# Softmax division on either of two engines, and a new order of work, in a hybrid RWKV / sliding-window attention step

## The chip, the cores and the metric

The kernel runs on one core of a Trainium2 chip. The metric is the time of one launch on the device in microseconds (us), the median of the runs. The engines are called as the profile calls them: PE (TensorE, matrix products; PEld its weight loads), DVE (VectorE), ACT (ScalarE), POOL (GpSimd) and SP (SyncE, which issues the DMAs).

## What is computed

One layer of a decoder, for a prompt of 2048 tokens and for eight single-token samples that share the weights. Cut to what matters:

```
mod = silu(c) @ w_ada + b_ada ; shift, scale, gate = split(mod, 3)
h = rms_norm(x) * (1 + scale) + shift
u = h @ w_in                                  # r, k, v, lora, z, q, k, v, two gates
o_a = rwkv(r, k, v, decay, a)                 # state recurrence in chunks of 64 tokens
logits = q @ k.T / 8 + bias(dist), masked to a window of 128
m = max(max(logits), sink) ; p = exp(logits - m)
probs = p / (sum(p) + exp(sink - m))          # the softmax with a sink
o_b = probs @ v
merged = sigmoid(g_a) * ((o_a * silu(z_a)) @ w_o_a) + sigmoid(g_b) * ((o_b * silu(z_b)) @ w_o_b)
y = x + gate * (merged @ w_out)
```

## The kernel before

The 2048 tokens are worked off in four quarters of 512 (`q` is 0 to 3; here first to fourth quarter). The eight samples ride along in the second. In a quarter, `make_h` norms the input (of the next quarter, ahead of time), `dense` makes each 128 columns of `h @ w_in` (a weight is split into two parts, and three products of 128x128 by 512 stand for one exact product), `rwkv_group` does the recurrence for two groups of heads (`half` 0 and 1: `prep_pair`, `inverses`, then a chain of eight chunk steps), `attention` works four blocks of 128 queries (`attend`), and `merge` and `finish` close the quarter. `STAGES` says in which order a quarter takes its two groups and the attention.

Ahead of it all, `ada` makes `mod` in six groups of 512 columns, four of them before the first quarter (`ADA`). A group takes eight loads of `w_ada` of 256 KB. Where its flag is False, each load is split by a cast (ACT or DVE) and a subtraction (DVE), and PE makes two products of 18x512 in the short form. Where it is True, PE multiplies the whole fp32 load with a 9-column operand, which it does in two records, and neither ACT nor DVE touches the load. Four small transposing products and an addition on DVE finish a group; `make_h` needs the groups 0 and 2 for its first half and 1 and 3 for its second.

The order of work is no loop order. The program records every operation with a key, and `schedule` places them before the build: for each engine, in turn, the ready operation with the smallest key. The key is six times the count of dense steps so far, less a lead from `LEADS` (a row per kind of work, eight numbers for the quarters and halves). Each engine then executes its list strictly in that order, so an operation that waits holds up all behind it. An operation may name two engines (`copy` names ACT and DVE, many products DVE and POOL), and `schedule` then takes the one that it finds free first. On PE, `schedule` prefers among ready products one that uses the array as the last one did, within `NEAR` units of key.

In `attend`, DVE adds the bias and takes the maximum (L1273), ACT takes eight exponentials with their sums (L1285), DVE inverts the sum, and then multiplies the eight 128x256 tiles by it (L1290, `ts`, always DVE). PE transposes the result (L1297), copies follow (L1299), and PE multiplies by the values (L1302).

Of the kernel before, what the change touches and what calls it, by code (L numbers as in the profile page):

```python
# [13 lines left out]
AF = mybir.ActivationFunctionType  # L14
ALU = mybir.AluOpType
# [72 lines left out]
def _constants():  # L88
# [19 lines left out]
CAPS = {"p": 92, "s": 11, "t": 14,  "nl": 1, "d": 3, "g": 5}  # L108
LEADS = {
    "prep": (2813.7, 2813.7, 2813.7, 3436.9, 2813.7, 2813.7, 3438.6, 2813.7),  # L110
    "inv": (2996.9, 2996.1, 5811.5, 5811.5, 3844.5, 4038.1, 3844.5, 3844.5),
    "chain": (1123.8, 1097.6, 888.3, 1123.8, 2826.9, 888.3, 888.3, 1097.6),
    "gn": (2855.6, 3576.9, 3664.2, 4278.9, 4097.0, 4097.0, 3576.9, 4278.9),
    "wd": (2660.8, 2660.8, 451.6, 3265.3, 1897.4, 1897.4, 1897.4, 1897.4),
    "norm": (6898.3, 3392.1, 820.0, 988.1, 462.2, 462.2, 838.5, 462.2),
    "att": (4680.1, 4566.4, 4726.2, 4726.2, 4352.4, 4352.4, 4902.9, 4642.8),
    "sample": (1353.8, 3662.2, 1353.8, 3662.2, 1353.8, 3662.2, 3662.2, 1353.8),
    "bias": (4326.4, 4447.3, 4335.8, 2812.3, 1723.9, 4335.8, 4355.1, 2812.3),
    "h": (3270.3, 3142.9, 3267.4, 3267.4, 3533.2, 3372.5, 3372.5, 3267.4),
    "x": (390.0, 390.0, 427.3, 427.3, 456.5, 456.5, 395.2, 427.3),  # L120
}
WLEAD, ELEAD = 5000.0, 6000.0
HGATE = 4
ADA = ((0, False), (1, True), (2, False), (3, False))
EARLY, PLACE = 1, 3
INORDER = 24
STAGES = ('0A1', '01A', '0A1', '0A1')
# [151 lines left out]
SWITCH = 50  # L279
FULL_ARRAY = (128, 128)  # L280
TURN = (0.09, 0.19)
NEAR = 300
AHEAD = 2
PE_LAT = 0.23

# [1 line left out]
def schedule(prog):  # L287
# [68 lines left out]
    def pick(e):  # L356
        T = free[e]
        best = None
        for x in ready[e]:
# [23 lines left out]
            if t <= T + 1e-9:  # L383
                if e == "pe" and table[1] not in (None, FULL_ARRAY, o.table[0]):
                    for y in ready[e]:
                        if y[0] > x[0] + NEAR:
                            break
# [87 lines left out]
def _free_size(v):  # L475
    n = 1
    for x in v.shape[1:]:
        n *= x
    return n


def _cost(e, op, out, ins, kw):
    n = _free_size(out)
    psum = any(v.buf.kind in ("d", "g") for v in ins)
    ptr = sum(1 for v in ins[1:] if _free_size(v) == 1 and n > 1)
    if e == "dve":
        if op == "tensor_mul" and any(len(v.ap.ap) > 2 and v.ap.ap[-1][0] >= 16 for v in ins):
            return 0.07 + n * 0.00178
        if op == "tensor_tensor_scan":
            return 0.07 + n * 0.00208  # L490
        if op in ("tensor_copy", "memset", "tensor_scalar"):
            return 0.067 + n * (0.00104 if psum else 0.00052) + 0.061 * ptr * (op == "tensor_scalar")
        if op == "tensor_reduce":
            return 0.07 + _free_size(ins[0]) * 0.00104
        if op == "reciprocal":
            return 0.07 + n * 0.0063
        return 0.07 + n * 0.00104 + 0.061 * ptr * (op == "scalar_tensor_tensor")
    if e == "act":
        return (0.052 if psum else 0.094) + n * 0.000833 + 0.093 * (len(ins) - 1 + ("accum_out" in kw))
    if op == "memset":  # L500
        return 0.035 + n * 0.00084
    if op == "tensor_scalar":
        return 0.147 + n * 0.0034
    if op == "tensor_copy":
        return 0.14 + n * 0.0008
    return 0.147 + n * 0.0022
# [3 lines left out]
def hybrid_step_kernel(ctx: ExitStack, tc: tile.TileContext, A, O):  # L510
    nc = tc.nc
# [4 lines left out]
    pr = Program(A["xT"].tensor, caps)  # L516
# [7 lines left out]
    def res(x):  # L524
        return x.real() if isinstance(x, View) else x
# [3 lines left out]
    def do(engs, op, out, /, *a, **k):  # L529

        if isinstance(engs, str):
            engs = {e: op for e in engs.split("/")}
        outs = [out] + ([k["accum_out"]] if "accum_out" in k else [])
        ins = [x for x in (*a, *(v for n_, v in k.items() if n_ != "accum_out")) if isinstance(x, View)]
        table = None
        if op == "activation":
            table = {AF.Ln: 5, AF.Exp: 0, AF.Tanh: 0}.get(a[1])
        o = pr.rec({e: _cost(e, n_, out, ins, k) for e, n_ in engs.items()},
                   lambda e: getattr(ENG[e], engs[e])(res(out), *(res(x) for x in a), **{n_: res(v) for n_, v in k.items()}),  # L539
                   outs, ins, table=table)  # L540
        if op in ("tensor_reduce", "memset", "transpose"):
            o.port = False
# [7 lines left out]
    def add(out, a, b, engs="dve"):  # L550
        do(engs, "tensor_add", out, a, b)
# [4 lines left out]
    def ts(out, in_, s1, s2, op0, op1=None, engs="dve"):  # L556
        k = {} if op1 is None else {"op1": op1}
        do(engs, "tensor_scalar", out, in_, s1, s2, op0=op0, **k)

    def stt(out, a, s, b, op0, op1):  # L560
        do("dve", "scalar_tensor_tensor", out, a, s, b, op0=op0, op1=op1)

    def act(out, in_, f, scale=1.0, bias=0.0, **k):
        do("act", "activation", out, in_, f, bias=bias, scale=scale, **k)
# [52 lines left out]
    def P(shape, dt=F32):  # L617
        return pr.tile("p", shape, dt)

    def Sm(shape):  # L620
        return pr.tile("s" if math.prod(shape[1:]) > 16 else "t", shape)

    def G(shape):
        return pr.tile("g", shape)
# [618 lines left out]
    def attend(q, n, qn, kk, kprev, vt, bt, zb):  # L1243
        k0 = 128 if (q == 0 and n == 0) else 0
        nk = 256 - k0
        lg = [[P([128, 2, 256]) for _ in range(2)] for _ in range(2)]
        mx = Sm([128, 8])
        for p2 in range(2):
            pss = [G([128, 2, 256]) for _ in range(2)]
            calls = []  # L1250
            for p in range(2):
                for g, h in enumerate((lo, hi)):
                    qs = qn[2 * p2 + p][g][:, n * 128:(n + 1) * 128]
                    if n == 0:
                        parts = [(kk, slice(0, 128), slice(128 - k0, 256 - k0))]
                        if q > 0:
                            parts.append((kprev, slice(0, 128), slice(0, 128)))
                    else:
                        parts = [(kk, slice(n * 128 - 128, n * 128 + 128), slice(0, 256))]
                    for t, cols, to in parts:  # L1260
                        calls.append((pss[g][:, p, to], qs, t[g][:, cols], dict(start=True, stop=False)))
                        calls.append((pss[g][:, p, to], qs, t[2 + g][:, cols], dict(start=False, stop=True)))
            mms(calls)
            for p in range(2):
                for g in range(2):
                    h = 4 * g + 2 * p2 + p
                    do("dve", "tensor_tensor_reduce", lg[g][p2][:, p, 0:nk], in0=pss[g][:, p, 0:nk],
                       in1=bt[g][p2][:, p, k0:256], scale=1.0, scalar=-3e38, op0=ALU.add, op1=ALU.max,
                       accum_out=mx[:, h:h + 1])
        do("dve", "tensor_max", mx, mx, vc("sinks", 0, 8))  # L1270
        nmx = Sm([128, 8])
        ts(nmx, mx, -1.0, None, ALU.mult)
        es = Sm([128, 8])  # L1273
        add(es, nmx, vc("sinks", 0, 8))
        act(es, es, AF.Exp)
        den = Sm([128, 8])
        for h in range(8):
            x = lg[h // 4][h % 4 // 2][:, h % 2, 0:nk]
            act(x, x, AF.Exp, bias=nmx[:, h:h + 1], accum_out=den[:, h:h + 1])
        add(den, den, es)  # L1280
        do("dve", "reciprocal", den, den)
        for h in range(8):
            x = lg[h // 4][h % 4 // 2][:, h % 2, 0:nk]
            ts(x, x, den[:, h:h + 1], None, ALU.mult)
        ops = G([128, 4, 128])  # L1285
        for kb in range(k0 // 128, 2):
            ptss = []
            for g in range(2):
                pt = G([128, 4, 128])
                for p in range(4):  # L1290
                    tr(pt[:, p, :], lg[g][p // 2][:, p % 2, kb * 128 - k0:kb * 128 - k0 + 128], ident)
                pts = P([128, 4, 128])
                copy(pts, pt)
                ptss.append(pts)
            v = vprev if n + kb == 0 else vt[:, n + kb - 1]
            mms([(ops[h], v[:, h], ptss[g], dict(start=(kb == k0 // 128), stop=(kb == 1)))
                 for g, h in enumerate((lo, hi))])  # L1297
        for p in range(4):
            y = zb[p][:, n * 128:n * 128 + 128]  # L1299
            mul(y, ops[:, p, :], y)  # L1300
# [236 lines left out]
    early = {}  # L1537
    for g, whole in ADA:
        if g == ADA[PLACE][0]:
            early = {key: weights("w_in", INDEX[key], "dve") for key in ORDER[:EARLY]}  # L1540
# [3 lines left out]
    for q in range(NQ):  # L1544
        sample = q == SQ
# [5 lines left out]
        x = shifted(("wd", 0))  # L1551
# [183 lines left out]
```

## Time and profile before

| | us |
|---|---|
| median of 3 runs | 1837.15 |
| lowest and highest of them | 1836.59, 1839.27 |
| profiled execution, own time | 1840.68 |
| its span | 1838.9 |

| engine | busy us | share |
|---|---|---|
| PE | 1785.1 | 97% |
| DVE | 1293.6 | 70% |
| ACT | 806.7 | 44% |
| POOL | 112.7 | 6% |

A busy PE is read with care: ends of products are modelled, and a product that runs at half clock or waits inside the pipeline counts as busy as well. What a stretch costs is better read from the distance between starts.

### The profile page before, as it was taken

The page shows a single profiled execution, that of the slowest core. Times are in us where ns is not written, and L with a number is a line of the kernel's source. Part 1 is how long each engine was busy: PE and PEld are TensorE (multiplying, and loading weights), DVE is VectorE, ACT ScalarE, POOL GpSimd, SP SyncE. Part 2 cuts the span into 40 slices and gives each one's busy share as a digit, 9 for nine tenths or more (in the row PEclk, how much of TensorE's full clock was granted, in tenths as well). Part 3 has the DMA queues.
Part 4 walks back from the last instruction along what each step waited for, and adds up shares of the span by engine and source line. Part 5 has one row for each costly group of instructions (what it writes and reads, how often), then busy time and mean ns, then how long its engine had stood idle before and what let it go on. Part 6 is the DMA issues. An engine that isn't in the chain of part 4 may idle for free.

```text
span 1838.9 us, 34113 instructions
## 1 busy us (share of the span) xinstructions
PE 1785.1 (97%) x12544; PEld 1436.3 (78%) x12544; DVE 1293.6 (70%) x3160; ACT 806.7 (44%) x1690; POOL 112.7 (6%) x191
## 2 busy tenths in 40 slices
PE   6999999999999998999999999999999999999999
PEld 2777766777898987999997786686888787777787
DVE  8989989587389967957527799673733879873251
ACT  6687645462263756235005765513303567431300
POOL 0100310000011100000000001100000100100000
PEclk9999999999999999999999999999999999999999
DMA  9677575858944534575465543445829263364626
GB/s 333 214 233 254 184 227 188 274 190 292 327 161 124 165 94 123 175 228 177 162 214 177 182 139 104 140 158 180 288 88 310 73 218 91 97 204 150 221 109 201
DMA packets 238933, 343.34 MB, mean 187 GB/s; under 512 B 73981, under 2 KB 77742, under 8 KB 238764
## 3 DMA queue, kind: packets, MB, share of 16 engines
q1 hardware_dynamic: 238764, 341.14, 56.4%
q8 instruction: 99, 1.62, 0.4%
q14 instruction: 70, 0.57, 0.1%
HBM read 263.09 MB, written 77.96 MB: 185 GB/s over the span
## 4 chain that ended last, share of the span: by engine, by line
PE 62%; DVE 13%; ACT 5%; DMA 3%; issue 2%; SPq 0%; DVEq 0%; ACTq 0%
PE d L580 50%; DVE p L539 12%; PE g L598 7%; ACT p L539 3%; PE g L580 3%; PE g L605 2%; ACT L539 2%; DMA p<-lo_w_in 1%; DMA d<-p 0%; DMA p<-in_lora 0%; SPq L614 0%; DMA p<-lo_w_out 0%; DVE s L539 0%; DMA p<-in_w_o 0%; DMA nl<-d 0%
## 5 line engine op out<-in xcount | busy, mean ns | idle before, releaser
L580 PE MATMUL d<-p,p 128*128 128x512 f32 (+2 forms) x7176 | 1475.5, 356 | 17.3 <-ACT p L539 14.9
L580 PEld LDWEIGHTS d<-p,p 128*128 128x128 f32 (+1 forms) x7176 | 1145.1, 188 | 229.5 <-ACT p L539 16.5
L539 DVE TENSOR_TENSOR p<-p,p 128x512 fp32r<-128x512 f32 (+6 forms) x702 | 429.0, 638 | 43.8 <-ACT p L539 35.2
L539 ACT CAST p<-p 128x512 fp32r<-128x512 f32 (+3 forms) x310 | 182.3, 613 | 161.8 <-DVE p L539 85.4
L598 PE MATMUL g<-p,p 128*64 128x64 f32 (+5 forms) x4000 | 230.5, 241 | 8.9 <-DVE p L539 5.0
L598 PEld LDWEIGHTS g<-p,p 128*64 128x64 f32 (+4 forms) x4000 | 175.1, 140 | 74.5 <-issue 20.6
L539 ACT COPY p<-g 64x128 f32<-64x128 f32 (+4 forms) x359 | 130.6, 372 | 150.9 <-PE g L598 78.9
L539 ACT ACTIVATE p<-d,vec 128x511 f32<-128x511 f32 (+1 forms) x65 | 39.2, 603 | 250.9 <-PE d L580 249.4
L539 ACT ACT_TABLE_LOAD x107 | 137.3, 1283 | 19.4 <-PE g L580 16.8
L539 ACT ACTIVATE p<-d 128x512 f32<-128x512 f32 (+1 forms) x120 | 61.4, 512 | 172.3 <-PE d L580 166.5
L539 DVE SCALAR_TENSOR_TENSOR p<-p,d 128x512 f32<-128x512 f32 (+1 forms) x120 | 69.6, 580 | 85.5 <-PE d L580 81.8
L539 DVE TENSOR_TENSOR p<-p,nl 128x2 f32<-128x2 f32 (+30 forms) x248 | 126.4, 510 | 4.4
L539 DVE SCALAR_TENSOR_TENSOR p<-d,modt,p 128x512 f32<-128x512 f32 (+2 forms) x40 | 25.8, 644 | 132.0 <-PE d L580 125.3
L539 DVE TENSOR_TENSOR p<-g,s 64x128 f32<-64x128 f32 (+1 forms) x124 | 40.4, 326 | 97.2 <-PE g L598 93.2
L539 ACT ACTIVATE p<-p 128x512 f32<-128x512 f32 (+2 forms) x161 | 98.1, 631 | 13.9 <-DVE p L539 7.3
L539 DVE TENSOR_TENSOR p<-g,cst 64x256 f32<-64x256 f32 (+1 forms) x192 | 89.5, 506 | 5.2 <-PE g L598 4.2
L539 DVE TENSOR_REDUCE p<-p 128x15 f32<-128x450 f32 (+30 forms) x252 | 88.9, 354 | 4.3
L580 PE MATMUL g<-p,blocks 128*128 128x512 f32 x204 | 80.5, 425 | 9.6 <-DVE p L539 5.8
L605 PE MATMUL g<-cst,p 128*128 128x128 f32 (+1 forms) x457 | 72.7, 282 | 10.2 <-DVE p L539 9.1
L539 POOL TENSOR_TENSOR p<-p,p 64x256 f32<-64x256 f32 (+2 forms) x49 | 56.0, 1154 | 375.8 <-DVE p L539 225.0
L605 PEld LDWEIGHTS g<-cst,p 128*128 128x128 f32 (+1 forms) x457 | 53.6, 143 | 32.6 <-DVE p L539 15.3
L539 ACT ACTIVATE p<-p,t 128x256 f32<-128x256 f32 (+1 forms) x129 | 63.0, 493 | 9.7 <-DVE t L539 9.6
(139 smaller groups left out, 901.2 us busy)
## 6 DMA issues: line engine op xcount, KB each, us to landing
p<-hi_w_in SPq DMA_DIRECT2D x258, 256.0 KB, 5.1
p<-lo_w_in SPq DMA_DIRECT2D x258, 256.0 KB, 5.3
p<-in_w_in SPq DMA_DIRECT2D x86, 256.0 KB, 3.8
hi_w_in<-p SPq DMA_DIRECT2D x86, 256.0 KB, 2.9
lo_w_in<-p SPq DMA_DIRECT2D x86, 256.0 KB, 2.6
p<-in_xT SPq DMA_DIRECT2D x64, 256.0 KB, 5.3
p<-in_w_ada SPq DMA_DIRECT2D x48, 256.0 KB, 5.3
p<-hi_w_o SPq DMA_DIRECT2D x48, 256.0 KB, 5.3
```

Of the source, the lines that this page charges most:

```text
L539: lambda e: getattr(ENG[e], engs[e])(res(out), *(res(x) for x in a), **{n_: res(v) for n_, v in k.items()}),
L580: pr.rec({"pe": mm_cost(out, lhsT, rhs)}, lambda e: nc.tensor.matmul(res(out), res(lhsT), res(rhs), **k), [out], [lhsT, rhs], table=(part( ...
L598: nc.tensor.matmul(res(out), res(lhsT), res(rhs), **k)
L605: pr.rec({"pe": 2 * _free_size(in_) / 2400.0 + 0.003}, lambda e: nc.tensor.transpose(res(out), res(in_), res(idn)), [out], [in_, idn], tab ...
```

## The change

The eight multiplications of `attend` by the inverted sum may now run on ACT as well as on DVE (`scaled`); the flag of two of the four early `ada` groups is True where it was False; `NEAR` is 4000 where it was 300; and 27 of the 88 numbers in `LEADS` are others, of which one row stands here.

```diff
 LEADS = {
...
-    "chain": (1123.8, 1097.6, 888.3, 1123.8, 2826.9, 888.3, 888.3, 1097.6),
+    "chain": (1123.8, 1208.2, 888.3, 1123.8, 609.1, 609.1, 888.3, 1097.6),
...
-ADA = ((0, False), (1, True), (2, False), (3, False))
+ADA = ((0, True), (1, True), (2, False), (3, True))
...
-NEAR = 300
+NEAR = 4000
...
+    def scaled(out, in_, s):
+
+        run_ = {"act": lambda: nc.scalar.activation(res(out), res(in_), AF.Copy, scale=res(s)),
+                "dve": lambda: nc.vector.tensor_scalar(res(out), res(in_), res(s), None, op0=ALU.mult)}
+        pr.rec({"act": _cost("act", "activation", out, [in_, s], {}), "dve": _cost("dve", "tensor_scalar", out, [in_, s], {})},
+               lambda e: run_[e](), [out], [in_, s])
...
         for h in range(8):
             x = lg[h // 4][h % 4 // 2][:, h % 2, 0:nk]
-            ts(x, x, den[:, h:h + 1], None, ALU.mult)
+            scaled(x, x, den[:, h:h + 1])
```

Lines from L560 on are seven higher in the changed kernel (L580 is L587, L598 L605, L605 L612). Of the 128 divisions, 45 come to ACT and 83 stay on DVE; PE goes from one shape of the array to another 539 times where it did 552 times.

The first place is PE's list at the start. `p_13` and `p_12` are the two forms of the conditioning operand (18 and 9 columns), `blocks` is the operand of the norm's sum in `make_h`. Before:

```order
L580 MATMUL d_209<-p_39_326,p_13_260 18x512
L580 MATMUL g_212<-p_41_330,blocks 128x512
L580 MATMUL d_209<-p_45_337,p_13_260 18x512
L580 MATMUL d_209<-p_43_334,p_13_260 18x512
L580 MATMUL g_212<-p_48_342,blocks 128x512
L580 MATMUL d_209<-p_52_352,p_13_260 18x512
```

Now:

```order
L587 MATMUL d_209<-p_15_268,p_12_256 9x512
L587 MATMUL d_209<-p_17_274,p_12_256 9x512
L587 MATMUL g_212<-p_41_329,blocks 128x512
L587 MATMUL g_212<-p_43_334,blocks 128x512
L587 MATMUL d_209<-p_19_279,p_12_256 9x512
L587 MATMUL d_209<-p_21_283,p_12_256 9x512
```

Groups 0, 1 and 3 are now whole products (9x512), and two of them stand ahead of both products of the norm.

The second place is ACT's list in the first quarter, where `inverses` of group 0 ends. The tiles of 32x512 and 32x8x32 are its copies (L1109 and L1115), for which PE waits; the casts of 128x512 split a weight that a DMA has just loaded. Before:

```order
L539 ACTIVATE p_614_2714<-d_210 128x512
L539 COPY p_590_2585<-g_214 128x512
L539 CAST p_623_2785<-p_615_2718 128x512
L539 CAST p_625_2792<-p_618_2727 128x512
L539 COPY p_627_2799<-g_215 32x512 x2
L539 COPY p_585_2558<-g_214 32x8x32
```

Now:

```order
L539 CAST p_580_2628<-p_571_2584 128x512
L539 ACTIVATE p_582_2636<-d_210 128x512
L539 COPY p_587_2678<-g_213 32x512 x2
L539 CAST p_594_2739<-p_585_2673 128x512
L539 COPY p_544_2444<-g_215 32x8x32
```

The two casts of the next weight stood ahead of the copies of 32x512; now the copies stand ahead of both.

The third place is PE's list in the third quarter, in the chain of chunk steps of group 0. Products of 64x64 are the chain, those of 128x512 dense work. Before, the end of a step and the start of the next:

```order
L598 MATMUL g_214<-p_2197_11609,p_2243_11849 64x64
L580 MATMUL d_211<-p_1947_10087,p_2488_13001 128x512
L580 MATMUL d_211<-p_1953_10123,p_2486_12994 128x512
L580 MATMUL d_211<-p_1955_10135,p_2486_12994 128x512
L580 MATMUL d_211<-p_1953_10123,p_2488_13001 128x512
L580 MATMUL d_211<-p_1959_10156,p_2486_12994 128x512
L580 MATMUL d_211<-p_1961_10170,p_2486_12994 128x512
L598 MATMUL g_214<-p_2196_11605,p_2205_11648 64x64
```

Now, the last dense products ahead of the start of a step:

```order
L587 MATMUL d_209<-p_1943_10173,p_2382_12595 128x512
L587 MATMUL d_209<-p_1945_10179,p_2380_12587 128x512
L587 MATMUL d_209<-p_1948_10193,p_2380_12587 128x512
L587 MATMUL d_209<-p_1945_10179,p_2382_12595 128x512
L587 MATMUL d_210<-p_1919_10035,p_2429_12888 128x512
L605 MATMUL g_216<-p_2164_11525,p_2173_11568 64x64
```

Six products of 128x512 stood between the two steps. Now 24 of them stand there (two with `blocks`, the norm's sum) and four transposes; at the ends of the next two steps 11 and 7 of them stand, where 4 stood.

## Rows read from the trace of the kernel before

**Rows 1.** The page: busy time of each engine, share of the span, instructions.

```profile
PE 1785.1 (97%) x12544; PEld 1436.3 (78%) x12544; DVE 1293.6 (70%) x3160; ACT 806.7 (44%) x1690; POOL 112.7 (6%) x191
```

**Rows 2.** Waits of PE, whole span: for whom, us in total, times, longest.

```profile
PE d L580 <- ACT p L539: 14.9, 3, 13.7
PE g L605 <- DVE p L539: 9.1, 10, 3.4
```

**Rows 3.** Chain that ended last: start, us, what; a stretch of dense products.

```profile
1722.02 112.73 PE d L580 x486
```

**Rows 4.** Groups by line and shape, softmax: count, busy us, mean ns, idle before.

```profile
L539 ACT ACTIVATE p<-p,t 128x256 f32<-128x256 f32 x120 | 59.5, 501 | 7.7 <-DVE t L539 7.5
...
L539 DVE TENSOR_SCALAR p<-p,t 128x256 f32<-128x256 f32 x120 | 34.2, 358 | 3.9 <-issue 3.8
```

**Rows 5.** Timeline from 0 to 75 us: start, us, engine, instruction, [idle before].

```profile
5.92 17.34 SPq L614 DMA_DIRECT2D p<-in_w_ada  x24
...
13.65 0.61 PE L580 MATMUL d<-p,p 128*18 128x512 f32 x1 [13.65 <-ACT p L539]
...
17.76 0.15 PEld L580 LDWEIGHTS d<-p,p 128*18 128x18 f32 x1 [0.28 <-DVE p L539]
...
18.19 0.15 PEld L580 LDWEIGHTS d<-p,p 128*18 128x18 f32 x1 [0.28 <-issue]
...
24.93 5.25 SPq L614 DMA_DIRECT2D p<-in_w_ada  x8
...
26.03 0.09 PEld L580 LDWEIGHTS d<-p,p 128*9 128x9 f32 x1 [0.34 <-issue]
26.46 0.09 PEld L580 LDWEIGHTS d<-p,p 128*9 128x9 f32 x1 [0.34 <-DMA p<-in_w_ada]
...
30.95 3.47 PE L580 MATMUL d<-p,p 128*18 128x512 f32 x14
...
44.62 1.05 PE L580 MATMUL g<-cst,p 18*128 18x9 f32 x8 [0.51 <-ACT p L539]
...
46.86 10.93 PE L580 MATMUL d<-p,p 128*128 128x512 f32 x46
```

**Rows 6.** The page, DMA issues: count, KB each, us from issue to landing.

```profile
p<-in_w_ada SPq DMA_DIRECT2D x48, 256.0 KB, 5.3
```

**Rows 7.** Timeline from 236 to 250 us, end of the inverses, first quarter.

```profile
239.75 1.65 PE L580 MATMUL d<-p,p 128*128 128x512 f32 x6
...
241.41 1.32 ACT L539 CAST p<-p 128x512 fp32r<-128x512 f32 x2 [4.56 <-DMA p<-in_w_in]
...
243.39 0.24 PE L598 MATMUL g<-p,p 32*32 32x32 f32 x2 [1.99 <-ACT p L539]
...
245.83 2.93 PE L580 MATMUL d<-p,p 128*128 128x512 f32 x6
```

**Rows 8.** Stretches: from:to, us, busy by engine (instructions), PEclk, DMA share, GB/s.

```profile
248.00:250.00 2.00, 2.00 (x8) 1.60 (x8) 1.97 (x8) 0.35 (x1) 0.00 (x0) 0.50 0.92 298
...
736.40:738.40 2.00, 2.00 (x11) 2.00 (x10) 2.00 (x7) 1.07 (x2) 0.00 (x0) 0.50 0.91 327
```

**Rows 9.** Timeline at 735 us, attention of the second quarter.

```profile
735.32 0.32 DVE L539 TENSOR_SCALAR p<-p,t 128x256 f32<-128x256 f32 x1 [3.79 <-issue]
735.34 0.09 DVE L539 MEMSET nl<- 128x32 f32 x1
...
735.69 1.11 PE L605 MATMUL g<-cst,p 128*128 128x128 f32 x4 [3.40 <-DVE p L539]
```

**Rows 10.** Timeline of PE from 80 to 113 us, first quarter.

```profile
90.94 0.74 PE L580 MATMUL g<-p,blocks 128*128 128x512 f32 x2 [1.53 <-DVE p L539]
```

**Rows 11.** Waits of PE from 1130 to 1180 us, third quarter.

```profile
PE g L598 <- DVE p L539: 3.1, 4, 1.5
PE g L605 <- DVE p L539: 1.0, 1, 1.0
```

**Rows 12.** Stretch in the attention of the third quarter, columns as in Rows 8.

```profile
1080.00:1100.00 20.00, 20.00 (x117) 16.74 (x117) 19.74 (x78) 12.60 (x48) 0.00 (x0) 1.00 0.29 93
```

More of the change, by code (lines that the diff above doesn't have):

```diff
@@ L110 @@
     "prep": (2813.7, 2813.7, 2813.7, 3436.9, 2813.7, 2813.7, 3438.6, 2813.7),
-    "inv": (2996.9, 2996.1, 5811.5, 5811.5, 3844.5, 4038.1, 3844.5, 3844.5),
-    "chain": (1123.8, 1097.6, 888.3, 1123.8, 2826.9, 888.3, 888.3, 1097.6),
-    "gn": (2855.6, 3576.9, 3664.2, 4278.9, 4097.0, 4097.0, 3576.9, 4278.9),
-    "wd": (2660.8, 2660.8, 451.6, 3265.3, 1897.4, 1897.4, 1897.4, 1897.4),
+    "inv": (2996.9, 2996.1, 5293.6, 5811.5, 5293.6, 4038.1, 5293.6, 5293.6),
+    "chain": (1123.8, 1208.2, 888.3, 1123.8, 609.1, 609.1, 888.3, 1097.6),
+    "gn": (3022.4, 3132.6, 3097.4, 3132.6, 3925.1, 3925.1, 3925.1, 3925.1),
+    "wd": (2660.8, 2660.8, 377.1, 377.1, 1897.4, 1897.4, 1897.4, 1897.4),
     "norm": (6898.3, 3392.1, 820.0, 988.1, 462.2, 462.2, 838.5, 462.2),
     "att": (4680.1, 4566.4, 4726.2, 4726.2, 4352.4, 4352.4, 4902.9, 4642.8),
[L117 to L120, printed above, removed]
+    "sample": (1353.8, 2341.0, 1353.8, 3662.2, 1353.8, 3662.2, 3662.2, 1353.8),
+    "bias": (4342.2, 4342.2, 4335.8, 2812.3, 1693.8, 1693.8, 1693.8, 2812.3),
+    "h": (4519.0, 4519.0, 3267.4, 3267.4, 3533.2, 3372.5, 3372.5, 3267.4),
+    "x": (390.0, 390.0, 427.3, 427.3, 462.2, 456.5, 395.2, 462.2),
 }
```

## Prediction

> **What bounds the kernel.** I read the page first: PE is busy 97% of the span, DVE 70%, ACT 44% [rows 1]. So time is won only where PE stands or runs slowly, or where it gets fewer or cheaper products. The waits of PE come next: they are small, 14.9 us for ACT (of which 13.7 is the first product's) and 9.1 us at the transposing products for DVE in ten waits [rows 2]. The chain that ended last then gives the price of dense work: 486 products of 128x512 take 112.73 us, 0.232 each [rows 3]. A stall costs more than its own length: behind the two stalls that I looked at, the stretches show a granted clock of 0.50, the 1.2 GHz level, in place of 1.00, 2.4 GHz [rows 8]. The change is therefore worth what it does to single stalls, and I found these by laying PE's new order beside the timeline of before.
>
> **The divisions.** Of 128, 45 go to ACT. On DVE one takes 0.358 us alone [rows 4] and 0.28 in a run (1.40 for five [rows 9]). ACT's price for a division is in no row; the nearest is its exponential with a sum on the same tile, 0.501 [rows 4], which I take, as the division has the same read and write and no sum. It may lie between 0.28, as fast as DVE, and 0.501. In a block of eight, some three go to ACT (1.5 us) while five stay on DVE (1.4 us), where eight took 2.2: the path from exponentials to transposes is some 0.8 us shorter. In 16 blocks that is 13 us, but PE has dense work to do meanwhile: all its waits for DVE at transposing products are 9.1 us [rows 2], so nearly all of it is hidden and I cost the division itself at 0. Without that cover, if divisions queue behind exponentials, PE waits; that is E below. The terms follow, in order of time.
>
> **T1, the start: +3.4 us (−1 to +6.2).** Two groups become whole products. Split, 14 records take 3.47 us [rows 5], so 16 take 4.0. A whole record starts 0.43 after the one before (26.03 and 26.46 [rows 5]), two make one product of 0.86, eight make 6.9. That is 3 us more for a group, 6 for two; PE's extra is at most 6.2 (with the split at 3.8). What is removed, 16 casts and 16 subtractions, PE did wait for there: 0.28 for DVE at 17.76, with records 0.43 apart, not 0.25 [rows 5]; and the first product waits to 13.65 for a cast, where a whole product needs the load alone. The loads are issued 0.72 apart from 5.92 on (17.34 for 24) and land 5.3 after issue [rows 5, 6]: the first at 12 to 13, the last early one (issue 24.93 + 5.25, landing 5.3 later) at 35.5. So PE, not the loads, paces the new start: from 13.0, 24 whole products at 0.86 (20.6), 16 split records (3.8), two norm sums (0.5), three sets of transposing products at 1.05 (3.2) and some 2 us for early products at half speed make 43.1; the bias and two dense products bring it to 44.3, and the row that the last set transposes comes from a copy now on DVE, at some 45. Then the last set ends at 46.3. Before it ended at 44.62 + 1.05 = 45.67, by when 12 more dense products had been made, 2.8 us. So +0.6 + 2.8 = +3.4. The low end is a start of PE at 12 and no cold products, the high one all of the extra products uncovered.
>
> **T2, shapes of the array: −1.5 (0 to −3.0).** There are 13 fewer switches. No row prices one; they cost from nothing to the slot of a dense product, 0.232 [rows 3]. I take half.
>
> **T3, first quarter, end of the inverses: −4.5 (−5 to 0).** Two casts for which a DMA is late hold ACT idle 4.56 us and end at 242.7; the copies that PE needs stand behind them, so PE waits 1.99 at 243.39 [rows 7] (and some 0.4 beside it). The clock is then 0.50 [rows 8], and six dense products take 2.93 where the same six took 1.65 before the stall [rows 7]; over the 6.6 us to 250 about 2.5 is lost so, if all of it was at half clock. 1.99 + 0.4 + 2.5 is 4.9. The new order has the copies ahead of both casts. What is late next is the weight itself: the dense products behind need those casts. They stand further behind, so I leave 0.4 for that.
>
> **T4, first quarter, 87 to 113 us: −2.0 (−3.4 to 0).** PE waits 1.53 at 90.94 [rows 10] for the squares of the next input's norm. With five smaller waits I count 3.4. The lead of `h` puts 11.1 us of PE work, at the prices of T1 and rows 3, where 7.9 stood between the matching operations; I take 60% of it.
>
> **T5, second quarter's attention: −2.0 (−4.8 to +1).** DVE stands 3.79 us [rows 9]: its list has the memset of `nl` ahead of six divisions (the two labels at 735.32 and 735.34 read as swapped), and that memset waits for the DMAs that write out what `nl` held. PE waits 3.40, and its clock is 0.50 after it [rows 8, 9]: together 4.8, with 1.4 for the 2.8 us at half clock. In the new list the divisions precede the memset, but a subtraction that a norm's product needs stands right behind it, with 0.5 us of PE work in hand. The wait thus mostly moves. I take 40% of the gain; a longer wait at the new place gives the +1.
>
> **T6, third quarter's chain: −3 (−4.7 to 0).** From 1130 to 1180 PE waits 3.1 us in the chain and 1.0 at transposes [rows 11], and a little for ACT. With 24, 11 and 7 products of 0.232 between steps in place of 6 and 4, the waits on the first steps are covered. These products are taken from elsewhere, so I leave a third.
>
> **T7, new waits: +4 (0 to +14).** In the second halves of the third and fourth quarter DVE is full: 19.74 of 20 us [rows 12]. There the PE work between a block's logits and its transposes falls from some 18 to 13 us in the new order, in four blocks. 16.74 of those 20 us are PE's [rows 12], so PE has some slack already; I take 1 us a block.
>
> **The sum:** 3.4 − 1.5 − 4.5 − 2.0 − 2.0 − 3 + 4 = −5.6. The profiled execution's 1840.68 becomes 1835.1; the median of the runs is 3.5 under the profiled one, so I forecast **1831.6**. A measurement of this kernel tells about 0.2%, 3.7 us, from no change.
>
> **The rivals.**
> - **A**, the forecast: −5.6, chance 0.47. T3 speaks for it most: its cause can be read in a row, and the order that makes it is gone.
> - **D**, no new waits: T7 is 0, as DVE is rid of 45 × 0.28 = 13 us; −9.6, 1827.5. If the gains of T5 and T6 also come whole (−2.8, −1.7), 1823. For it speaks the shorter path of a block; against it DVE's 19.74 of 20 [rows 12]. 0.13.
> - **C**, no change that can be told: the start takes all of +6.2, and the memset's wait re-forms whole (T5 is 0): −5.6 + 2.8 + 2.0 = −0.8, 1836.3. This is also the case where the option does little, as 83 of 128 divisions stay and PE never waited for most of them. For it: PE paces the new start. Against it: 16 subtractions less on DVE there. 0.26.
> - **E**, slower: in those four blocks the divisions on ACT stand behind the exponentials and copies in ACT's list (ACT has 12.60 of 20 already [rows 12]), and the cover that fell by 5 us is no longer enough. The price is up to 5 us a block, 20 in all; at 3.5 a block T7 is 14, the sum is −9.6 + 14 = +4.4, 1841.6. It decides from 13.3 us on, 3.3 a block. For it: the cut in cover is in the order. Against it: ACT has 7 of 20 us free there. 0.14.
>
> The Trainium skill (page "ScalarE: Activation LUTs", section "Rules for kernel authors") says that a multiplication belongs on VectorE and not on ScalarE; the tile's rows, 0.501 on ACT for an exponential against 0.358 on DVE [rows 4], agree in direction. By that rule alone, with 45 × 0.14 = 6.4 us all on the path, the forecast would be +0.8, 1838.0; I count it under E, since ACT is the engine with room.
>
> **How the numbers follow.** Faster by over 0.2% holds A and D, 0.60; within it C, 0.26; slower E, 0.14. The range goes from D with its whole gains, 1823, to just short of E, 1841. A's own range, with T5, T6 and T7 off by some 1 each (1.7 together), is 1829.9 to 1833.3.
>
> **What would show it.** T1: eight more pairs of 9x512 in each of two groups, and the last set of transposing products of the start ends near 46.3. T3: no wait near 2 us at the 32x32 products that end the inverses, and a clock of 1.00 behind it. T5: no wait of 3.4 at the transposes of the second quarter, perhaps one at a norm's product instead. T6: less than 2 us of waits for DVE in the third quarter's chain. T7: transposing products (now L612) that wait under 2 us each for DVE or ACT in the third and fourth quarter. The prediction is wrong if the sum of PE's waits does not fall, if a new stall with a clock of 0.50 behind it appears, or if the last early set ends after 50.

## The result, and the profile after

The changed kernel takes 1851.59 us (median of 4 runs, 1849.97 to 1853.26), beside 1838.21 for the kernel before in the same comparison. The ratio on record is 1.0064: 0.64% slower, with an interval of 0.52 to 0.77%; the two medians by themselves lie 13.4 us apart. The forecast was 1831.6, faster, with a range to 1841: wrong in sign and outside its range. The profiled execution takes 1852.02, its span 1850.0, 11.1 us more than before; the profiled execution of the kernel before, at 1840.68, was 2.5 us above the median.

The page, busy time of each engine (before: [rows 1]):

```profile
PE 1792.8 (97%) x12544; PEld 1440.6 (78%) x12544; DVE 1287.0 (70%) x3142; ACT 804.0 (43%) x1689; POOL 103.5 (6%) x178
```

PE is busy for 7.7 us longer, DVE 6.6 us less. ACT is busy no longer although it has 45 divisions more: by the two pages, 18 casts (most of them of the two `ada` groups) and 28 copies fewer run on it. PE's waits sum to 50.4 us where they summed to 47.6; a second profile (`a_again`, below) has 53.1. Shares of busy time tell nothing of the cause here.

To find the place, I laid the traces side by side. Each has 4520 PE records of 128x128 by 512 (dense work, and the norm's sums), and the n-th of one is set against the n-th of the other. Between the rows the order differs, so that only rows at the end of a stage, where both have done the same work, are read. Differences of start to the kernel before in us, with the sum of the prediction's forecasts for its terms up to there (T2 left out) and, in the last column, a second profile of the changed kernel from the experiments:

| at (us, before) | stage that ends | changed | terms | changed, again |
|---|---|---|---|---|
| 78 | start | +2.35 | +3.4 (T1) | +3.28 |
| 221 | first quarter, early | +0.49 | +1.4 (T4) | +1.22 |
| 510 | first quarter | −0.29 | −3.1 (T3) | −0.13 |
| 985 | second quarter | +7.65 | −5.1 (T5) | +5.27 |
| 1071 | third, before its second half | +6.22 | −5.1 | +3.85 |
| 1474 | third quarter | +8.11 | −6.1 (T6, half of T7) | +5.86 |
| 1830 | end | +11.08 | −4.1 (half of T7) | +8.80 |

So the whole loss arises behind the first quarter. The largest step lies at 735 us, at the memset of `nl` that T5 speaks of. The timeline of the changed kernel there (DVE, PE, and SP's loads of `nl`):

```profile
726.30 0.43 DVE L539 CAST p<-p 128x512 fp32r<-128x512 f32 x1 [2.40 <-ACT p L539]
736.62 0.66 DVE L539 TENSOR_TENSOR p<-p,p 128x512 fp32r<-128x512 f32 x1 [9.89 <-issue]
736.64 0.09 DVE L539 MEMSET nl<- 128x32 f32 x1
...
727.02 0.73 PE L587 MATMUL g<-p,blocks 128*128 128x512 f32 x2
737.33 0.79 PE L587 MATMUL g<-p,blocks 128*128 128x512 f32 x1 [9.58 <-DVE p L539]
...
732.05 1.13 SPq L621 DMA_DIRECT2D nl<-d  x2
```

PE now waits 9.58 us where it waited 3.40 [rows 9]. As the prediction said, the divisions are out of the memset's way and the subtraction of a norm stands behind it (the labels of the two are swapped again). What it had wrong is the length. The memset does not wait for `nl` to be written out, as T5 had it, but for loads into it (`nl<-d`, back from DRAM): it can start when these, issued from 732.05 on, have landed, which is at 736.6 here and was at 735.3 before. DVE reaches it at 736.62 − 9.89 = 726.7, where it came at 735.32 − 3.79 = 731.5 before. So 4.8 us of the 6.1 that the wait grew are DVE's earlier arrival, and 1.3 the data's later one.

The place of T3's stall, the waits of T4, the last early `ada` set, and the clock, in the changed kernel (PE, and one row of DVE):

```profile
12.66 3.57 PE L587 MATMUL d<-p,p 128*9 128x512 f32 x4 [12.66 <-DMA p<-in_w_ada]
...
44.48 1.05 PE L587 MATMUL g<-cst,p 9*128 9x9 f32 x8
...
89.90 0.47 PE L587 MATMUL g<-p,blocks 128*128 128x512 f32 x1 [1.37 <-DVE p L539]
...
246.95 0.68 DVE L539 TENSOR_TENSOR p<-p,t 128x512 f32<-128x512 f32 x1
...
247.68 0.66 PE L612 MATMUL g<-cst,p 128*128 128x128 f32 x4 [1.83 <-DVE p L539]
...
603.09 1.53 PE L587 MATMUL g<-t,p 64*128 64x8 f32 x8 [0.63 <-ACT t L539]
```

```profile
248.00:250.00 2.00, 2.00 (x9) 1.60 (x7) 1.98 (x7) 1.17 (x2) 0.00 (x0) 0.63 0.93 300
...
604.00:606.00 2.00, 2.00 (x9) 1.98 (x10) 2.00 (x7) 1.97 (x3) 2.00 (x3) 0.50 1.05 400
```

The second fence is the view of stretches (columns as in rows 8). The waits of 1.99 and 0.36 at the inverses [rows 7] are gone, and a wait of 1.83 stands 4 us behind their place, with the clock below full speed after it. It is at four transposes of the recurrence (`prep_pair`), which wait for the multiplication at 246.95; no division of the softmax runs between 193 and 685 us. At 604 us the clock is at 0.50, the lower of its two levels, behind a wait of 0.63 that before had too, without it.

In the second halves of the third and the fourth quarter, waits that rows 11 do not have (PE, changed kernel):

```profile
1130.40 0.91 PE L612 MATMUL g<-cst,p 128*128 128x128 f32 x4 [0.48 <-DVE p L563]
...
1156.20 0.47 PE L587 MATMUL g<-p,blocks 128*128 128x512 f32 x1 [0.91 <-DVE p L539]
1163.44 0.66 PE L612 MATMUL g<-cst,p 128*128 128x128 f32 x4 [0.95 <-DVE p L539]
1176.51 0.66 PE L612 MATMUL g<-cst,p 128*128 128x128 f32 x4 [1.02 <-DVE p L539]
...
1592.15 0.47 PE L587 MATMUL g<-p,blocks 128*128 128x512 f32 x1 [0.91 <-DVE p L539]
1599.38 0.66 PE L612 MATMUL g<-cst,p 128*128 128x128 f32 x4 [0.95 <-DVE p L539]
1612.43 0.65 PE L612 MATMUL g<-cst,p 128*128 128x128 f32 x4 [1.07 <-DVE p L539]
```

From 1060 to 1210 us PE's waits sum to 4.7 (before: 4.7), from 1490 to 1650 to 4.7 (before: 2.4). The first row is the longest wait for a division in the third quarter (L563 and L562 are the divisions on DVE and ACT); the fourth has one of 0.48 as well. All other rows stand behind the attention, whose last divisions end at 1132 and 1568 us: they are sums over `blocks`, and transposes that are not the softmax's, where neither T7 nor E looked for a wait.

### The profile page after: what moved, and what is told of

The parts are those of the page before. It is cut to its first block, busy times and chain, and to the rows that moved or that the text cites. A ratio compares the mean times of both kernels' runs of the same rounds, so it can differ in the third digit from the quotient of the medians.

```text
span 1850.0 us, 34051 instructions
## 1 busy us (share of the span) xinstructions
PE 1792.8 (97%) x12544; PEld 1440.6 (78%) x12544; DVE 1287.0 (70%) x3142; ACT 804.0 (43%) x1689; POOL 103.5 (6%) x178
## 4 chain that ended last, share of the span: by engine, by line
PE 59%; DVE 14%; ACT 5%; DMA 4%; issue 2%; SPq 0%; DVEq 0%; ACTq 0%
PE d L587 49%; DVE p L539 13%; PE g L605 5%; ACT p L539 4%; PE g L587 3%; ACT L539 1%; DMA out_vws<-p 1%; DMA p<-lo_w_in 1%; PE g L612 1%; DMA p<-lo_w_out 1%; DVE p L563 0%; DVE t L539 0%; DMA p<-in_cv 0%; DMA p<-hi_w_in 0%; DMA p<-in_w_o 0%
## 5 line engine op out<-in xcount | busy, mean ns | idle before, releaser
L587 PE MATMUL d<-p,p 128*128 128x512 f32 (+2 forms) x7176 | 1479.2, 357 | 15.2 <-DMA p<-in_w_ada 12.7
L587 PEld LDWEIGHTS d<-p,p 128*128 128x128 f32 (+1 forms) x7176 | 1146.9, 188 | 228.7 <-DVE p L539 20.0
L539 DVE TENSOR_TENSOR p<-p,p 128x512 fp32r<-128x512 f32 (+6 forms) x690 | 417.7, 631 | 66.4 <-ACT p L539 48.5
L539 ACT CAST p<-p 128x512 fp32r<-128x512 f32 (+3 forms) x292 | 172.9, 614 | 162.9 <-DVE p L539 90.1
L605 PE MATMUL g<-p,p 128*64 128x64 f32 (+5 forms) x4000 | 229.3, 241 | 5.1 <-ACT p L539 2.0
L605 PEld LDWEIGHTS g<-p,p 128*64 128x64 f32 (+4 forms) x4000 | 176.0, 140 | 70.7 <-issue 25.1
L539 ACT COPY p<-g 64x128 f32<-64x128 f32 (+5 forms) x331 | 121.1, 370 | 145.6 <-PE g L612 61.4
L587 PE MATMUL g<-p,blocks 128*128 128x512 f32 x204 | 80.0, 423 | 19.2 <-DVE p L539 16.4
L539 DVE TENSOR_REDUCE p<-p 128x12 f32<-128x276 f32 (+30 forms) x252 | 88.8, 353 | 4.0
L612 PE MATMUL g<-cst,p 128*128 128x128 f32 (+1 forms) x457 | 70.6, 279 | 12.6 <-DVE p L539 10.5
L612 PEld LDWEIGHTS g<-cst,p 128*128 128x128 f32 (+1 forms) x457 | 51.6, 140 | 36.5 <-DVE p L539 16.0
```

Of the source, the lines that this page charges most:

```text
L587: pr.rec({"pe": mm_cost(out, lhsT, rhs)}, lambda e: nc.tensor.matmul(res(out), res(lhsT), res(rhs), **k), [out], [lhsT, rhs], table=(part( ...
L605: nc.tensor.matmul(res(out), res(lhsT), res(rhs), **k)
L612: pr.rec({"pe": 2 * _free_size(in_) / 2400.0 + 0.003}, lambda e: nc.tensor.transpose(res(out), res(in_), res(idn)), [out], [in_, idn], tab ...
```

## The experiments

Times are ratios to the kernel before, in the same comparison, with their 95% intervals; the changed kernel is at 1.0064. Differences in us between two of them are the difference of the ratios by 1839.

**Moving the memset alone.** After the planner is done, each memset of `nl` is moved behind, right ahead of the first instruction that reads `nl`; nothing else moves on any engine. Once in the changed kernel (`a_late`), once in the one before (`b_late`). (`diag` is the list of these memsets, `z.succ` what needs one.)

```diff
     order = schedule(pr)
+    for z in diag:
+        order.remove(z)
+        order.insert(min(order.index(u) for u in z.succ), z)
```

> The changed kernel with one thing moved: each memset of nl (the diagonal behind a DRAM round trip) stands in DVE's list right ahead of the first instruction that reads nl; PE's and ACT's lists are the same. Theory (the memset near 727 us blocks DVE for 9.9 us, PE waits 9.6 and then runs at half clock for some 7 us): the wait of 9.6 falls under 3, and the time falls by 6 to 11 us, to 1841 to 1846. Rival (PE has used up its work by then and would wait for the round trip anyway): a wait of 5 us or more stays near 730 to 745, and the time falls by under 3 us, 1849 or more.

> The kernel before with the same move of the nl memsets, other lists the same. Theory: the wait of 3.4 us at 735 and the half clock after it go, the time falls by 3 to 5 us, to 1833 to 1835. Rival (the wait moves to the next use of nl): under 1.5 us.

Measured: `a_late` 1.0041 (1.0028 to 1.0054), some 4 us faster than the changed kernel; `b_late` 0.9995 (0.9986 to 1.0004), no difference that can be told. Timelines of the two, DVE and PE of `a_late`, then PE of `b_late`:

```profile
737.97 0.09 DVE L540 MEMSET nl<- 128x32 f32 x1 [5.13 <-DMA nl<-d]
738.56 0.16 DVE L540 TENSOR_TENSOR p<-p,nl 128x2 f32<-128x2 f32 x1 [0.51 <-DMA p<-in_idl]
738.64 0.68 DVE L540 TENSOR_TENSOR p<-p,s 128x512 f32<-128x512 f32 x1
...
740.84 0.42 DVE L540 CAST p<-p 128x512 fp32r<-128x512 f32 x1
...
741.31 0.80 PE L588 MATMUL g<-p,blocks 128*128 128x512 f32 x1 [5.42 <-DVE p L540]
```

```profile
744.85 0.27 PE L606 MATMUL g<-cst,p 64*128 64x64 f32 x1 [1.92 <-DVE p L540]
```

```profile
746.00:748.00 2.00, 2.00 (x14) 2.00 (x12) 1.90 (x7) 0.55 (x1) 0.00 (x0) 0.53 0.89 323
748.00:750.00 2.00, 2.00 (x10) 2.00 (x11) 1.67 (x5) 0.80 (x3) 0.00 (x0) 0.50 0.02 6
```

In `a_late` the wait of PE falls from 9.58 to 5.42: still the rival's figure (5 or more), while the time lies between the two forecasts. The memset's place was some 4 us of it. The rest is DVE's order too, at least in part: DVE stands 5.13 us for the loads of `nl`, and PE's product then waits for the cast at 740.84, which does not read `nl` but stands behind its first readers. What moving these as well would give was not tried. `b_late` shows why a wait of this kind is worth less than its length. By the aligned products it gains 4.8 us on the kernel before from 708 to 743 us and has given back 3.8 by 769, in a shorter wait and another stretch at half clock (the last fence, stretches).

**The engine alone, the order fixed.** In `a_dvediv` the changed kernel keeps its order, and the 45 divisions of ACT run on DVE at the same places. In `b_actdiv` the kernel before keeps its order, and the divisions of heads 2, 5 and 7 (48 in all) run on ACT. (`divs` is the list of the divisions, `z.on` the engine of one.)

```diff
     order = schedule(pr)
+    for z in divs:
+        z.on = "dve"
```

```diff
     order = schedule(pr)
+    for z, h in divs:
+        if h in (2, 5, 7):
+            z.on = "act"
```

> The changed kernel in the same order, but the 45 divisions that ScalarE took run on VectorE at the same places. Theory (the engine of the division hardly matters, the order does): within 2 us of the changed kernel's 1851.6. Rival (divisions on ScalarE stand behind exponentials and hold the transposes): faster by 5 us or more, 1846 or less. If it is slower by over 3 us, the option is worth something by itself.

> The kernel before in its own order, with three of the eight divisions of each block (48 of 128) on ScalarE at the same places; PE's list is the same. Theory (in a fixed order the lighter VectorE shortens the way to the transposes, but PE waits only some 9 us there in all): faster than before by 0 to 4 us, 1835 to 1839. Rival (divisions wait behind what stands ahead of them in ScalarE's list): slower by 2 us or more.

Measured: `a_dvediv` 1.0102 (1.0088 to 1.0116), 7 us slower than the changed kernel; `b_actdiv` 1.0040 (1.0026 to 1.0054), slower than before. My theory failed in both, and rival E with it as the cause of the result: in the changed order the divisions on ACT are what keeps the loss from being larger, and its trace has no wait for a division over 0.48 us in the last two quarters. In the order of before they do what E said. DVE and PE of `b_actdiv` in the third quarter:

```profile
1097.98 0.17 DVE L540 TENSOR_TENSOR t<-t,t 128x8 f32<-128x8 f32 x1 [1.29 <-ACT p L540]
...
1098.40 1.31 PE L613 MATMUL g<-cst,p 128*128 128x128 f32 x10 [0.43 <-ACT p L563]
...
1110.39 0.76 PE L613 MATMUL g<-cst,p 128*128 128x128 f32 x5 [0.60 <-ACT p L563]
```

A division (L563 in `b_actdiv`) stands between the exponentials of the next block; DVE waits 1.29 us for the sums of these, then PE for DVE and ACT. By the aligned products the divisions cost 3.4 us in the attention of the third quarter and as much in that of the fourth. So each of these two lists fits the engines that it was made for, and the price of an engine change has no sign by itself.

**The start alone.** `b_ada` is the kernel before with the new ADA, `a_ada` the changed kernel with the old; both differ from their parent in the first quarter's lists only.

```diff
-ADA = ((0, False), (1, True), (2, False), (3, False))
+ADA = ((0, True), (1, True), (2, False), (3, True))
```

> The kernel before with the new ADA alone; the lists differ from those of before only up to some 300 us, behind that they are word for word the same. Theory (start +3.2 us by the aligned dense products, of which the first quarter's new order gives some back): 0 to +3.5 us, 1838 to 1842. Rival (whole products are the main cause of the 13.4 us): +7 us or more, 1845 or more.

> The changed kernel with the old ADA; the lists differ in the first quarter alone. Theory (the whole products cost 2 to 3 us of PE's time at the start, and the new lead of h takes care of what else they do): faster than the changed kernel by 1 to 4 us, 1848 to 1851. Rival (the new leads need the new ADA, as the new ADA needed the new leads): slower by 5 us or more, with a wait of PE of several us where the second quarter begins, at some 420 us.

Measured: `b_ada` 1.0094 (1.0079 to 1.0110), `a_ada` 1.0071 (1.0059 to 1.0083). Neither does what the theory said. At the start they do: at 78 us `b_ada` is 3.1 us behind the kernel before, and `a_ada` 2.9 ahead of the changed kernel (2.35 + 0.55), the size of T1. But at the end of the first quarter `b_ada` is 14.8 us behind, and `a_ada` 5.8 behind the changed kernel. PE of `b_ada`, at the first dense work on the next quarter's norm:

```profile
428.48 8.23 PE L580 MATMUL d<-p,p 128*128 128x512 f32 x24 [8.26 <-ACT p L539]
```

**The second quarter's cause.** `a_q2` is the changed kernel with the old leads of the second quarter (inv, gn, wd); `b_near` the kernel before with NEAR at 4000; `b_scaled` the kernel before with the choice of the division's engine and nothing else.

```diff
-            ts(x, x, den[:, h:h + 1], None, ALU.mult)
+            scaled(x, x, den[:, h:h + 1])
```

> The changed kernel with the leads of the second quarter (inv, gn, wd of its two halves) put back to the old values; the lists differ from the changed kernel's in the second quarter alone. Theory (two thirds of the loss is in the second quarter, by its new leads: half clock at 602 to 610 and 650 to 657, the wait of 9.6 us at 727): faster than the changed kernel by 4 to 9 us, 1843 to 1848. Rival (NEAR and the division's choice spoil the second quarter, not the leads): within 2 us of 1851.6.

> The kernel before with NEAR at 4000 alone; the lists differ in the second quarter alone, with 8 fewer or more changes of the array's shape. Theory (changes of shape are worth little, the order of the second quarter decides): between 4 us faster and 4 us slower, with any difference in the waits and the half clock between 600 and 760 us. Rival (NEAR is what spoils the second quarter): slower by over 5 us.

> The kernel before with the choice of the engine for the division alone, old leads, ADA and NEAR. Theory (VectorE is full in the attentions, so the choice gives several us by itself, as the 8 us in the other order say): faster than before by 2 to 7 us, 1832 to 1838. Rival (the order that follows it makes new waits of the same size): within 2 us of before, or slower.

Measured: `a_q2` 1.0069 (1.0057 to 1.0081), so the leads of the second quarter are not the cause; `b_near` 1.0023 (1.0015 to 1.0032); `b_scaled` 1.0069 (1.0054 to 1.0083), which loses 7.0 us in the first quarter and 4.5 in the second. PE in `b_scaled`, near 740 us:

```profile
741.23 3.70 PE L587 MATMUL g<-p,p 128*64 128x129 f32 x16 [9.48 <-DVE p L539]
```

The wait is there with the old leads, the old ADA and the old NEAR. In every list that was made with the choice in the second quarter, and in which the memset was not moved, it is 8.1 to 10.3 us (`a_q2` the least, the changed kernel again the most; `a_dvediv`, which has the order but not the engine, 9.08). In lists made without the choice PE's longest wait for DVE there is at most 3.7. It comes with the order that follows from the choice.

**The leads of the last two quarters.** `a_q34` is the changed kernel with the old leads of the third and fourth quarter, `b_q34` the kernel before with the new ones.

```diff
-    "inv": (2996.9, 2996.1, 5293.6, 5811.5, 5293.6, 4038.1, 5293.6, 5293.6),
-    "chain": (1123.8, 1208.2, 888.3, 1123.8, 609.1, 609.1, 888.3, 1097.6),
+    "inv": (2996.9, 2996.1, 5293.6, 5811.5, 3844.5, 4038.1, 3844.5, 3844.5),
+    "chain": (1123.8, 1208.2, 888.3, 1123.8, 2826.9, 888.3, 888.3, 1097.6),
...
```

> The changed kernel with the leads of the third and fourth quarter put back to the old values; the lists are the changed kernel's up to the end of the second quarter. Theory (the new leads of chain and inverses in these quarters make waits at the softmax transposes and cost 5 us by the aligned products, +2.0 in the third and +3.0 in the fourth): faster than the changed kernel by 3 to 6 us, 1845.5 to 1848.5. Rival (any order of the planner for these quarters, made with the choice of the engine, loses that much): within 2 us.

> The kernel before with the new leads of the third and fourth quarter alone; its first two quarters are word for word the same. Theory (these leads move dense products from the steps of the attention to those of the chain; without the division's choice it is as in the changed kernel in the old division's place, where the two quarters lost 10 us): slower than before by 4 to 12 us, 1843 to 1851. Rival (the leads are good by themselves): within 2 us, or faster.

Measured: `a_q34` 1.0023 (1.0013 to 1.0034), 7.5 us faster than the changed kernel; `b_q34` 1.0025 (1.0016 to 1.0034). The theory holds in direction both ways, and `a_q34` gains more than it said. The waits that go are not at the softmax's transposes, as the theory had it, but behind the attention. PE's waits of `a_q34` from 1490 to 1650 us:

```profile
1545.23 0.55 PE L612 MATMUL g<-cst,p 128*128 128x128 f32 x3 [0.31 <-ACT p L562]
1602.93 0.66 PE L612 MATMUL g<-cst,p 128*128 128x128 f32 x4 [0.37 <-DVE p L539]
```

That is 0.7 us in place of 4.7; from 1060 to 1210 it is 1.9 in place of 4.7. So 6.8 us of waits go. By the aligned products of the two profiles, 5.9 us of the gain arise behind 985 us, where the lists differ; 2.4 lie ahead of it, where they are the same, and come with fewer stretches at half clock.

**The same lists again.** `a_again` is the changed kernel for a second profile.

> The changed kernel once more, for a second profile of the same lists. If the granted clock falls by chance where PE has waited, the stretches at half clock (602 to 610, 650 to 657, 728 to 743 us) stand elsewhere in part, and the span differs by some us with the waits the same to 0.1 us; if they belong to the lists, they come again at the same places.

It took 1849.72 us, span 1847.7. PE at 248 and 603 us and the stretches behind:

```profile
248.12 0.66 PE L612 MATMUL g<-cst,p 128*128 128x128 f32 x4 [1.83 <-DVE p L539]
...
603.22 1.06 PE L587 MATMUL g<-t,p 64*128 64x8 f32 x8 [0.62 <-ACT t L539]
```

```profile
248.00:250.00 2.00, 1.88 (x11) 1.63 (x11) 2.00 (x8) 1.08 (x2) 0.00 (x0) 1.00 0.97 315
...
604.00:606.00 2.00, 2.00 (x18) 1.98 (x18) 2.00 (x7) 1.97 (x3) 2.00 (x3) 1.00 1.01 355
```

The wait at 603 is the same (0.62, 0.63), the clock is at its upper level where it was at 0.50, and 2.1 of the 2.3 us between the two spans arise between 589 and 628 us. The stretches at half clock at 650 and from 728 on came again; the one at 248 did not, behind the same wait of 1.83. Three more runs have PE's list of the changed kernel up to the third quarter, and the same wait at 603 (0.61 to 0.63): `a_late` has the stretches at 603 and 650, `a_q34` half of that at 603 and none at 650, `a_q34_late` neither. Only the stretch at the long wait near 735 is in all five. So 2 of the 11 us were chance, not the lists.

**Three that close it.** `a_sc34`: the changed kernel with the choice in the third and fourth quarter alone. `b_sc34`: the kernel before with the choice there alone. `a_q34_late`: the changed kernel with both single repairs.

```diff
-            scaled(x, x, den[:, h:h + 1])
+            if q >= 2:
+                scaled(x, x, den[:, h:h + 1])
+            else:
+                ts(x, x, den[:, h:h + 1], None, ALU.mult)
```

> The changed kernel, with the choice of the division's engine in the third and fourth quarter alone (VectorE in the first two); from the third quarter on its lists are the changed kernel's. Theory (the order that comes with the choice is what empties PE in the second quarter): the wait for VectorE near 735 us is under 6 us, and the time is 3 us or more below the changed kernel's, under 1848.5. Rival (the new leads and NEAR do it): the wait of 8 us or more stays, and the time is within 2 us of 1851.6 or above it.

> The kernel before with the choice of the division's engine in the third and fourth quarter alone; the first two quarters are before's, the last two those of the kernel with the choice and old leads, where two quarters took 0.2 us less than before's, 2 us of half clock at 1454 us included. Theory (with leads made for them, the choice gains a little where VectorE is full): faster than before by 0 to 2.5 us, 1836.5 to 1839. Rival (the choice does no good with old leads): slower by 2 us or more.

> The changed kernel with the leads of the third and fourth quarter put back and the nl memsets moved behind. Theory (two separate causes): the 8.1 and 3.7 us of the two single edits add up, 1851.6 - 11.8 = 1839.8, 1838 to 1842, which is before's time. Rival (half clock and new waits eat one of them): 1843 or more.

Measured: `a_sc34` 1.0143 (1.0124 to 1.0162), the slowest of all; `b_sc34` 0.9998 (0.9989 to 1.0008); `a_q34_late` 1.0005 (0.9995 to 1.0016). PE in `a_sc34`, end of the first quarter and second:

```profile
430.51 7.99 PE L587 MATMUL d<-p,p 128*128 128x512 f32 x24 [8.28 <-ACT p L539]
...
742.74 0.58 PE L587 MATMUL d<-p,p 128*128 128x260 f32 x1 [2.81 <-DMA p<-hi_w_in]
```

In the second quarter the theory holds: without the choice there is no wait of 9 us (2.81 is left, for a weight). The quarter still loses 4.5 us to the kernel before, so the wait is not all of its loss; the rest was not traced. The time that the theory gave is wrong, because without the choice in the first quarter the wait of `b_ada` is back, 16.4 us at 510 us: the new ADA needs the order that comes with the choice, and the choice needs the new ADA (`b_scaled` and `a_ada`, 7.0 and 5.5 us behind the kernel before there). Together, with that quarter's new leads, they cost nothing there (−0.3); no run has the two without these leads. `a_q34_late` adds the two repairs, 1.0064 − 0.0023 − 0.0041 = 1.0000, measured 1.0005: with the memset moved and the old leads in the last quarters, the change is worth nothing that can be told, either way. None of these versions is faster than the kernel before.

## Why the prediction was wrong, step by step

- **What bounds the kernel**: right, as far as the differences were traced: each is a wait of PE, or the clock behind one.
- **The divisions at 0**: wrong. In a fixed order, 45 of them on ACT are worth 7 us in the changed kernel, and 48 cost as much in the one before. ACT's price was right: 0.502 us in the group below, taken as 0.501. By the Trainium skill's rule (page "ScalarE: Activation LUTs", section "Rules for kernel authors") multiplications belong on VectorE; `b_actdiv` agrees, 7 us the wrong way on ScalarE, and `a_dvediv` does not, 7 us the wrong way on VectorE.

```profile
L539 ACT ACTIVATE p<-p,t 128x256 f32<-128x256 f32 x120 | 59.7, 502 | 13.8 <-DVE t L539 13.6
...
L563 DVE TENSOR_SCALAR p<-p,t 128x256 f32<-128x256 f32 x79 | 22.7, 344 | 0.2
...
L562 ACT ACTIVATE p<-p,t 128x256 f32<-128x256 f32 x41 | 19.0, 502 | 3.9 <-DVE t L539 3.8
```

- **T1**: right. +2.35 and +3.28 in two profiles, forecast +3.4; the last set of the start begins at 44.48 and ends at 45.5, forecast 46.3. What `b_ada` loses beyond that was no part of the changed kernel.
- **T2**: not resolved. No run has the switches alone.
- **T3**: failed. The wait at the inverses went as the order said, but "what is late next" was taken to be the weight, at 0.4 us, and it was DVE: transposes outside the softmax wait for it, 0.89 at 224.99 and 1.83 at 247.68. From 221 to 300 us PE's waits sum to 2.7 us (3.6 in the second profile) where they summed to 2.4. From 221 to 510 us the gain is 0.8 and 1.3 in the two profiles, forecast 4.5, and even that is not the order's: the half clock behind the old stall does not come every time. `b_q34` has before's lists there and the wait at the inverses, the clock stays at 1.00, and it gains 2.2 us on the kernel before between 221 and 300 us.

```profile
244.12 0.24 PE L598 MATMUL g<-p,p 32*32 32x32 f32 x2 [1.64 <-ACT p L539]
```

```profile
246.00:248.00 2.00, 2.00 (x11) 1.59 (x12) 2.00 (x6) 1.22 (x4) 0.00 (x0) 1.00 0.41 122
```

- **T4**: right in sum (1.9 and 2.1, forecast 2.0): from 78 to 113 us the waits sum to 1.6 where they were 3.4. The largest of them, the 1.53 at 90.94 [rows 10] that the term was built on, is still 1.37 at 89.90; the smaller ones went.
- **T5**: the step that failed most. The memset waits for loads into `nl`, not for a write-out, which changes no number. I counted "0.5 us of PE work in hand" and still let the longer wait end at +1, since I had measured the new wait from the old one. It should have been counted from the new arrival of DVE and PE to the landing of `nl`. The quarter took +5.4 to +7.9 for −2.0 (the larger figure with the 2 us of chance); some 4 us of it are the memset's place (`a_late`).
- **T6 and T7**: +4.9 in both profiles (from 1071 us to the end) for +1. The waits of the chain went and the same sum came back at other transposes and at sums over `blocks` in the third quarter, 2.3 us more in the fourth. Of the 4.9, 1.9 arise in the third quarter, where the waits are no longer than before; these were not traced to rows. T7 looked in the wrong place, the softmax's transposes (0.48 us at most), and took slack for granted by a misread row: in [rows 12] PE is busy for all 20.00 us, and 16.74 is the share of the weight loads (PEld). `a_q34` shows that the new leads make the loss, and in which direction, not which of the leads.
- **The rivals**: C had the mechanism of T5, a wait that re-forms, at a price of nothing; E had the sign, by a mechanism that the runs exclude here (`a_dvediv`, and the waits for divisions above).

The sum: T5 missed by 7.4 or more, T3 by 3 to 4, T6 and T7 by 4, less 1.4 that the kernel before lost to the clock at 1012 us alone. That is about the forecast's −4.1 (without T2) to +8.8 or +11.1. Two of the signs that the prediction named came up: PE's waits did not fall in sum, and a longer stall with a clock of 0.50 behind it stands at 737 us. Open is why an order made with the choice brings DVE to the memset earlier: every plan made with the choice in that quarter has it, and no run took the planner apart. That the memset is placed too early at all has a likely reason in the kernel: `schedule` reckons 2.0 us for a DMA to land (`DMA_LAT`), and the load of `nl` took 4.1 from issue to landing in the kernel before. No run changed that number.

## What to carry to other kernels

A wait that moves is priced at its new place: from when the engines get there to when the data lands, never from its old length; the cover in between is read from the new order, in front of the wait and behind it. Where one list is made from many numbers, the parts of a change do not add: two that cost 7 and 15 us alone in the first quarter cost nothing there together with its new leads, so each should be tried both alone and taken out. An edit of the finished order (one instruction moved, one engine changed) tells a cause; a new plan from other inputs tells only whether that plan is better.

## What was not expected of the hardware

With the same lists and the same wait of 0.63 us, TensorE's granted clock fell to 0.50 for some 7 us in one profile and stayed at 1.00 in another, worth 2.1 us. `a_late` and `a_q34_late` have PE's list in common up to the third quarter: the first, with stretches at 605 and 653, loses 3.9 us to the kernel before through the second quarter, the other, without them, 0.5. The kernel before has such stretches at 244, 736, 750 and 1012 us; `b_ada`, which has its lists from the second quarter on, has them at 618, 676, 756 and 768, and is 3.4 us later through that quarter alone. Over 21 runs of one comparison the kernel before took 1836.05 to 1844.21 us. In this kernel, then, a single profile cannot settle a difference under some 4 us.
